# A decoder layer on one core: Strassen's gate over even and odd token tiles, the first weight tile in two column parts, buffers of gate, down and the out stage laid anew

## The chip, the core and the metric

The kernel runs on one core of one Trainium2 chip. The metric is the device time of one execution, in microseconds. Before the change the median of three runs is 3316.95 us (3312.92 to 3322.59).

## The reference

One layer of a decoder, for 1024 tokens of width 1024, all in float32: a SwiGLU block, a token mixer (an mLSTM branch and an RWKV-7 branch that two gates merge), and a second SwiGLU block, with a layer norm behind each.

```python
def swiglu(x, w_gate, w_up, w_down):
    return (jax.nn.silu(x @ w_gate) * (x @ w_up)) @ w_down
...
for l in range(DEPTH):
    x = layer_norm(ALPHA * x + 0.5 * swiglu(x, ffn1_w_gate[l], ffn1_w_up[l], ffn1_w_down[l]), ln1_g[l], ln1_b[l])
    mix = token_mixer(x, w_in[l], ...)
    x = layer_norm(ALPHA * x + mix, ln2_g[l], ln2_b[l])
    x = layer_norm(ALPHA * x + 0.5 * swiglu(x, ffn2_w_gate[l], ffn2_w_up[l], ffn2_w_down[l]), ln3_g[l], ln3_b[l])
```

The weights `w_gate` and `w_up` are 1024 x 2816 (22 column tiles of 128), `w_down` is 2816 x 1024.

## The kernel before, in words

**Numbers.** A float32 product is made of three fp32r products. `split` (L128) cuts a tile into a high part (a cast on ACT) and a low part (source minus high, on POOL or on DVE: `lo_eng`), and `mm3` (L148) issues high times high, high times low and low times high on TensorE (PE). So each operand costs a cast and a subtraction, and each product three matmuls, nearly all of 128x512.

**Stages.** In order of time: the gate of ffn1 (gate and up, to about 475 us), its down (to about 775), the mixer (B and C), the out stage D (`mix_out`, layer norm 2; about 2380 to 2562), the gate of ffn2 (to about 3034), its down with layer norm 3, and the end.

**The gate.** `gate_up` (L284) computes for one column tile f the gate and up of all tokens by Winograd's form of Strassen: the tokens in two halves (tiles 0 to 3 and 4 to 7) and the depth in two halves give a 2x2 block product with 7 products instead of 8, 84 matmuls instead of 96. The seven sums of token blocks are made once for a stage: `put_sums` (L222) adds and subtracts on DVE, and `put` (L211) transposes each sum on PE (L216, four 128x128 transposes), casts the high part on ACT (L219) and takes the low part from PSUM on DVE (L220). `weights` (L264) makes the seven sums of the weight blocks for each f (`tw` tiles, DVE, L266) and splits them, the low parts on POOL. The results come through `e` tiles: DVE adds (L288), a Silu on ACT, two products (L313, L318), and two 128x512 stores to h in DRAM (L315, L319). The stores go through SP's queue, those of the last f through ACT's. In both gates the first two products of the first two f's are "led" (`lead`): they need only the first half's plain blocks, and so run while the other sums are still being made.

**The down.** `down_all` (L355) takes the token tiles in groups of 3, 3 and 2. For each of the 22 f's it loads a piece of h (`hr`, L365) and two halves of a row block of `w_down` (`rw`, L371), splits them (`hr` with its low part on DVE, `rw` with its low parts on DVE and POOL in turn), and accumulates in PSUM. At a group's end DVE adds the sums to the residual (L390). The layer norms of a group (`layer_norm`, L420) are popped into the loop of the next group, one each third f; it works on pairs of tiles: statistics, a subtraction of the mean on ACT (L430), a product with gamma on POOL (L431), a chain of small DVE operations for the inverse root (L160 to L164, tiles `lnr` and `rst`), and a DVE operation of 128x1024 for each tile (L440). In the first down each normed tile is transposed too (`to_T`, L173 to L177).

**Buffers and queues.** `rw` (8), `tw` (6), `wr` (14) and `e` (18) are rings of 128x512 tiles. SP issues nearly all loads and stores in program order, and an entry whose buffer isn't free holds all behind it. The mixer's first loads of `w_in` (`raw`, `rawf`, L143) stand where their buffers let them, in before at the end of the first gate.

Of the kernel before, what the change touches and what calls it, by code (L numbers as in the profile page):

```python
# [16 lines left out]
P = 128  # L17
# [13 lines left out]
class Net:  # L31
    def __init__(self, ctx, tc, ins, out):
        self.ctx, self.tc, self.nc, self.I, self.out = ctx, tc, tc.nc, ins, out
        tp = lambda **kw: ctx.enter_context(tc.tile_pool(**kw))
        self.cp = tp(name="cp", bufs=1)
        self.gp = {}
        self.sp = self.rp = None
        self.pp = tp(name="pp", bufs=1, space=PSUM)
        self.dp = tp(name="dp", bufs=1, space=bass.MemoryType.DRAM)
        self.n = 0  # L40
# [7 lines left out]
    RING = {"rw": (8, F32), "tw": (6, F32), "wr": (14, F32R), "e": (18, F32)}  # L48
# [11 lines left out]
    def ring(self, tag, n=512):  # L60

        bufs, dt = self.RING[tag]
        return (self.ep if tag == "e" else self.rp).tile([P, 512], dt, tag=tag, bufs=bufs, name=self.nm(tag))[:, :n]
# [135 lines left out]
    def sums_pool(self, name):  # L199

        return self.pool(name)

    def sums(self, pool, a=None):
        big = lambda: pool.tile([P, NK, 512], F32R, tag="xq", bufs=3, name=self.nm("xq"))
        a, b = a or self.new_xT(), self.new_xT()
        c, d = (big(), big()), big()
        lo4, hi4 = slice(0, 4), slice(4, 8)
        return [self.cut(a, ALL, lo4), self.cut(a, ALL, hi4), self.cut(b, ALL, lo4), self.cut(b, ALL, hi4),
                self.cut(c, ALL, lo4), self.cut(c, ALL, hi4), (d[:, lo4], d[:, hi4])]
# [12 lines left out]
    def put_sums(self, cmb, a1, a2, s1):  # L222

        tt_ = self.nc.vector.tensor_tensor
        banks = "acdc"
        for p in range(4):
            tt_(s1[p], a2[p][0], a2[p][1], op=ALU.add)
            tt_(a2[p][0], a1[p][0], a2[p][0], op=ALU.subtract)
            tt_(a1[p][0], s1[p], a1[p][0], op=ALU.subtract)
            self.put(cmb[2], p, a1[p][0], banks[p])  # L230
        for i, t in ((3, lambda p: a2[p][0]), (4, lambda p: s1[p]), (5, lambda p: a2[p][1])):
            for p in range(4):
                self.put(cmb[i], p, t(p), banks[p])
        for p in range(4):
            tt_(a1[p][1], a1[p][1], a1[p][0], op=ALU.subtract)
            self.put(cmb[6], p, a1[p][1], banks[p])

    def prod(self, ps, w, x, first):
        for k in range(4):
            self.mm3(ps, self.cut(w, ALL, k), self.cut(x, ALL, k), first and k == 0, k == 3, not first)  # L240

    def lead(self, cmb, w1, w2):

        X, X2 = self.ps("g"), self.ps("b")
        self.prod(X, w1, cmb[0], True)
        self.prod(X2, w2, cmb[1], True)
        return X, X2

# [15 lines left out]
    def weights(self, b11, b12, b21, b22, led):  # L264
# [4 lines left out]
        if not led:  # L269
            out[0] = self.cut_w(b11)  # L270
# [3 lines left out]
        if not led:  # L274
            out[1] = self.cut_w(b21)
# [8 lines left out]
    def gate_up(self, cmb, f, ws, hD, led=None):  # L284
# [3 lines left out]
        add = lambda o, a, b: nc.vector.tensor_tensor(o, a, b, op=ALU.add)  # L288
        pr = lambda ps, i, first: self.prod(ps, ws[i], cmb[i], first)
        p1, sg0 = self.ring("e"), self.ring("e")  # L290
        if led:
            nc.scalar.copy(p1, led[0])
            add(sg0, led[1], p1)
            nc.scalar.activation(sg0, sg0, AF.Silu)
        else:
            X = self.ps("g")
            pr(X, 0, True)
            nc.scalar.copy(p1, X)
        u2, u3, up1, sg1, up0 = (self.ring("e") for _ in range(5))
        Y, Z = self.ps("b"), self.ps("c")  # L300
        pr(Y, 2, True)
        add(u2, Y, p1)
        if not led:
            pr(X, 1, False)
            nc.scalar.activation(sg0, X, AF.Silu)
# [8 lines left out]
        dma = (nc.scalar if f == NF - 1 else nc.sync).dma_start  # L314
        dma(hD[f * P:(f + 1) * P, 512:1024], up1)  # L315
# [3 lines left out]
        dma(hD[f * P:(f + 1) * P, 0:512], up0)  # L319

    def gate_first(self, pre, src, cmb, hD):

        nc = self.nc

        def get(r, c):
            ts = [self.ring("e") for _ in range(4)]
            for p in range(4):
                nc.sync.dma_start(ts[p], src[(4 * r + p) * P:(4 * r + p + 1) * P, c * 512:(c + 1) * 512])
            return ts

        B = [[None] * 4 for _ in range(2)]
        raws = lambda f, n, i: [B[f].__setitem__(i + 2 * k, self.raws(pre, f, k, (n,))[0]) for k in range(2)]
        a11 = get(0, 0)
        raws(0, "gate", 0)
        a12 = get(0, 1)
        raws(1, "gate", 0)
        a21 = get(1, 0)
        raws(0, "up", 1)
        a22 = get(1, 1)
        raws(1, "up", 1)  # L340
        for p in range(4):
            self.put(cmb[0], p, a11[p], "acdc"[p])
        for p in range(4):
            self.put(cmb[1], p, a12[p], "acdc"[p])
        led = [self.lead(cmb, self.cut_w(B[f][0]), self.cut_w(B[f][2])) for f in range(2)]
# [1023 lines left out]
```

## Time and profile before

| what | value |
|---|---|
| median of three runs | 3316.95 us |
| the profiled execution | 3316.42 us, its span 3314.7 us |
| mean granted TensorE clock | 0.967 |
| PE busy | 3100.1 us (94%) |
| DVE, ACT, POOL busy | 1984.5, 1085.7, 998.1 us |
| steady gate, 128x512 matmuls in 100 us | 432 |

The span is nearly the sum of PE's work and of the gaps in it, so it is read by its gaps: how long PE is idle in each stage, and what ended each wait. In the view by stretches each engine has its busy time and its number of instructions; in the view of waits a row names the waiting engine, the tile and line that waited, what released it, and the sum, count and longest of the waits.

### The profile page before, as it was taken

How to read it: one execution, taken by the hardware profiler on the slowest of the kernel's cores; microseconds unless marked ns; L12 is line 12 of the kernel's file. 1: busy time of each engine (PE TensorE's matmuls, PEld its weight loads, DVE VectorE, ACT ScalarE, POOL GpSimd, SP SyncE). 2: the span in 40 equal slices, each digit the busy share in tenths (PEclk: the TensorE clock that was granted, in tenths of full speed). 3: DMA queues.
4: the chain of work that ended last, by engine and by line, in shares of the span. 5: the costliest groups of instructions: out<-in, count | busy, mean ns of one | idle time of the engine just before them, and what ended most of it. 6: DMA issues, size and time to landing. Idle time of an engine off the chain costs nothing. (4 is left out here: it accounts for less than half of the span.)

```text
span 3314.7 us, 44985 instructions
## 1 busy us (share of the span) xinstructions
PE 3100.1 (94%) x15720; PEld 2495.2 (75%) x15720; DVE 1984.5 (60%) x4654; ACT 1085.7 (33%) x1790; POOL 998.1 (30%) x975
## 2 busy tenths in 40 slices
PE   7999989988899899999989999999999699999997
PEld 5888867777677777787877777777777588887785
DVE  6444435674657666757576766476568744444658
ACT  4333323443312222313232322375333333333434
POOL 3444433343212222222222122200002344443334
PEclk9999999999989999999998999999999899999998
DMA  3222237552222322322232223474562322224564
GB/s 121 80 86 83 77 107 234 185 189 66 58 69 64 77 78 57 78 60 76 66 73 64 74 77 93 129 234 143 178 232 83 108 82 77 80 86 156 167 200 164
DMA packets 457001, 365.37 MB, mean 110 GB/s; under 512 B 109981, under 2 KB 368711, under 8 KB 456775
## 3 DMA queue, kind: packets, MB, share of 16 engines
q1 hardware_dynamic: 449287, 348.87, 35.2%
q0 software_dynamic: 4608, 8.39, 0.9%
q10 hardware_dynamic: 2880, 5.24, 0.4%
q8 instruction: 124, 2.03, 0.3%
q14 instruction: 102, 0.84, 0.1%
HBM read 281.66 MB, written 80.74 MB: 109 GB/s over the span
## 5 line engine op out<-in xcount | busy, mean ns | idle before, releaser
L150 PE MATMUL psg<-xT,wf 128*128 128x512 f32 x2340 | 641.5, 410 | 0.7 <-ACT f L871 0.7
L134 POOL TENSOR_TENSOR wr<-rw,wr 128x512 fp32r<-128x512 f32 x260 | 345.2, 1328 | 511.2 <-ACT wr L130 450.4
L150 PEld LDWEIGHTS psg<-xT,wf 128*128 128x128 f32 x2340 | 429.1, 192 | 76.4 <-ACT f L871 1.1
L130 ACT CAST wr<-rw 128x512 fp32r<-128x512 f32 x392 | 242.1, 621 | 497.0 <-PE psc L150 253.5
L150 PE MATMUL psa<-xT,w 128*128 128x512 f32 x1200 | 316.4, 406 | 13.7 <-DVE pj L507 10.6
L134 POOL TENSOR_TENSOR wr<-tw,wr 128x512 fp32r<-128x512 f32 x176 | 233.9, 1331 | 303.6 <-ACT wr L130 303.6
L150 PE MATMUL psb<-xT,wr 128*128 128x512 f32 x1080 | 271.3, 401 | 15.6 <-ACT wr L130 10.7
L150 PEld LDWEIGHTS psa<-xT,w 128*128 128x128 f32 x1200 | 222.7, 192 | 64.8 <-DVE pj L507 15.3
L288 DVE TENSOR_TENSOR e<-psb,e 128x512 f32<-128x512 f32 x136 | 94.0, 691 | 293.3 <-PE psb L150 293.3
L150 PE MATMUL psc<-xq,wr 128*128 128x512 f32 x1056 | 260.5, 395 | 0.0
L150 PEld LDWEIGHTS psb<-xT,wr 128*128 128x128 f32 x1080 | 206.1, 191 | 66.6 <-ACT wr L130 11.5
L150 PE MATMUL psg<-wr,wr 128*128 128x512 f32 x792 | 213.9, 403 | 36.5 <-DVE wr L134 14.9
L150 PE MATMUL psg<-xT,wr 128*128 128x512 f32 x984 | 243.3, 396 | 1.5 <-ACT xT L219 1.5
L150 PEld LDWEIGHTS psc<-xq,wr 128*128 128x128 f32 x1056 | 199.4, 189 | 46.3
L150 PEld LDWEIGHTS psg<-xT,wr 128*128 128x128 f32 x984 | 186.1, 189 | 44.8 <-ACT xT L219 1.9
L130 ACT CAST wr<-tw 128x512 fp32r<-128x512 f32 x176 | 108.7, 621 | 327.1 <-PE psb L150 231.5
L150 PE MATMUL psb<-wr,wr 128*128 128x512 f32 x792 | 212.1, 405 | 0.0
L150 PEld LDWEIGHTS psg<-wr,wr 128*128 128x128 f32 x792 | 150.5, 192 | 75.3 <-DVE wr L134 18.8
L134 DVE TENSOR_TENSOR wr<-hr,wr 128x384 fp32r<-128x384 f32 (+1 forms) x132 | 163.7, 1240 | 47.6 <-ACT wr L130 41.4
L134 POOL TENSOR_TENSOR wf<-rawf,wf 128x512 fp32r<-128x512 f32 x100 | 133.3, 1349 | 179.2 <-ACT wf L130 154.3
L150 PEld LDWEIGHTS psb<-wr,wr 128*128 128x128 f32 x792 | 156.2, 198 | 33.7
L134 DVE TENSOR_TENSOR wr<-rw,wr 128x512 fp32r<-128x512 f32 x132 | 100.6, 762 | 134.2 <-PE psc L150 107.8
(369 smaller groups left out, 5190.6 us busy)
## 6 DMA issues: line engine op xcount, KB each, us to landing
rw<-in_ffn_w_down_dram SPq DMA_DIRECT2D x264, 256.0 KB
rawf<-in_w_in_dram SPq DMA_DIRECT2D x98, 256.0 KB
rw<-in_ffn_w_gate_dram SPq DMA_DIRECT2D x88, 256.0 KB
rw<-in_ffn_w_up_dram SPq DMA_DIRECT2D x88, 256.0 KB
h<-e SPq DMA_DIRECT2D x84, 256.0 KB
hr<-h SPq DMA_DIRECT2D x88, 192.0 KB
raw<-in_w_in_dram SPq DMA_DIRECT2D x50, 256.0 KB
qkD<-f SPq DMA_DIRECT2D x32, 256.0 KB
```

Of the source, the lines that this page charges most:

```text
L130: nc.scalar.copy(hi, src)
L134: eng.tensor_tensor(lo, src, hi.bitcast(F32), op=ALU.subtract)
L150: self.nc.tensor.matmul(out, a[u], b[v], start=first and i == 0, stop=last and i == 2, skip_group_check=more)
L288: add = lambda o, a, b: nc.vector.tensor_tensor(o, a, b, op=ALU.add)
```

## The change

What it does:

- Strassen's token halves are the even and the odd tiles instead of the first and the last four. `put_sums` then works for one pair of tiles at a time: four DVE sums and seven transposed sets for a pair.
- The first f of each gate is computed in two column parts: columns 0 to 255 (pairs 0 and 1) and 256 to 511 (pairs 2 and 3). In the first gate the second two pairs are loaded and summed after the first part in program order. The led products are gone.
- h is stored in pieces of 128x128, eight DMAs for an f instead of two, since the halves are interleaved in h.
- The ring of `e` has 14 buffers instead of 18; `wr` has a pool of its own in the first gate and another in the first down; `lng`, `hr` and `lnb` get their places at the start of the down.
- In the down both low parts of `rw` are taken on DVE; POOL takes none. The product with gamma moves from POOL to DVE, for all three layer norms.
- The mixer's first `w_in` loads are issued after the load of `w_down` for f = 17 of the third group.
- D: the eight `y` tiles have a pool of their own, `unit` tiles go from 18 to 10, gamma and beta are loaded at D's start, nothing is led, and no tile is transposed in the layer norm's callback; `put_sums` runs for the four pairs after `mix_out`.

The diff, cut to its core:

```diff
-    RING = {"rw": (8, F32), "tw": (6, F32), "wr": (14, F32R), "e": (18, F32)}
+    RING = {"rw": (8, F32), "tw": (6, F32), "wr": (14, F32R), "e": (14, F32)}
...
-    def put_sums(self, cmb, a1, a2, s1):
+    def put_sums(self, cmb, p, a1, a2, s1):
         tt_ = self.nc.vector.tensor_tensor
...
+        self.put(cmb[0], p, a1[0], "a")
+        tt_(s1, a2[0], a2[1], op=ALU.add)
+        tt_(a2[0], a1[0], a2[0], op=ALU.subtract)
+        self.put(cmb[1], p, a1[1], "c")
+        tt_(a1[0], s1, a1[0], op=ALU.subtract)
+        self.put(cmb[2], p, a1[0], "d")
+        self.put(cmb[3], p, a2[0], "c")
+        tt_(a1[1], a1[1], a1[0], op=ALU.subtract)
+        self.put(cmb[4], p, s1, "a")
+        self.put(cmb[5], p, a2[1], "c")
+        self.put(cmb[6], p, a1[1], "d")
...
-        dma = (nc.scalar if f == NF - 1 else nc.sync).dma_start
-        dma(hD[f * P:(f + 1) * P, 512:1024], up1)
+        hv = hD[f * P:(f + 1) * P, :].rearrange("r (p e t) -> r e p t", e=2, t=P)
+        dma = (nc.scalar if f == NF - 1 else nc.sync).dma_start
+
+        def store(e, t):
+            for p in range(c0 // P, c1 // P):
+                dma(hv[:, e, p], t[:, p * P - c0:(p + 1) * P - c0])
...
+        pair(0)
+        pair(1)
+        ws = self.weights(*B)
+        self.gate_up(cmb, 0, ws, hD, 0, 256)
+        pair(2)
+        pair(3)
+        self.gate_up(cmb, 0, ws, hD, 256, 512)
+        self.gate_rest(pre, cmb, hD, 1)
...
+            if f == 0:
+                self.gate_up(cmb, f, ws, hD, 0, 256)
+                self.gate_up(cmb, f, ws, hD, 256, 512)
...
+                    if (t0, f) == (6, 17):
+                        self.loaded = dma
                     d = self.ring("wr"), self.ring("wr")
-                    self.split(raw, *d, lo_eng=("dve", "pool")[c])
+                    self.split(raw, *d, lo_eng="dve")
...
-        nc.gpsimd.tensor_tensor(y[tt], y[tt], gb, op=ALU.mult)
+        nc.vector.tensor_tensor(y[tt], y[tt], gb, op=ALU.mult)
...
-    with net.phase("D", UB=18, VB=5, side="right"):
-        net.mix_out(net.hmT, y, fin2, load_y, load_ln)
-        a = x2T[0]
-        led = [net.lead([net.cut(a, ALL, k) for k in k4], *(net.cut(w, ALL, k) for k in k4)) for w in led]
+    with net.phase("D", UB=10, VB=5, side="right"):
+        load_ln()
+        v = [net.half() for _ in range(5)]
+        yt = [net.s("y", [P, D], bufs=8) for _ in range(8)]
+        y.extend(yt[4:] + yt[:4])
+        net.mix_out(net.hmT, y, fin2, load_y)
...
+            for p in range(4):
+                net.put_sums(cmb, p, *([y[2 * p + e][:, c] for c in c2] for e in range(2)), net.half())
...
-        net.rwkv_small(x1T)
-        with net.low():
-            for f in net.fillers(x1T):
-                f()
+        with tc.issue_after(net.loaded.ins):
+            net.rwkv_small(x1T)
+            with net.low():
+                for f in net.fillers(x1T):
+                    f()
```

How the program's order moves, at three places. The first is SP's queue at the very start, behind the first loads of x (`e`) and weights (`rw`); before:

```order
L328 DMA e_122<-in_x_dram 128x512
L328 DMA e_123<-in_x_dram 128x512
L328 DMA e_124<-in_x_dram 128x512
L328 DMA e_125<-in_x_dram 128x512
L253 DMA rw_130<-in_ffn_w_up_dram 128x4x128
L253 DMA rw_132<-in_ffn_w_up_dram 128x4x128
L328 DMA e_134<-in_x_dram 128x512
L328 DMA e_135<-in_x_dram 128x512
L328 DMA e_136<-in_x_dram 128x512
L328 DMA e_137<-in_x_dram 128x512
```

and after the change, where 13 to 18 of the queue are the weights of f = 1 and two small loads, and these follow:

```order
L241 DMA rw_762<-in_ffn_w_gate_dram 128x4x128
L241 DMA rw_764<-in_ffn_w_up_dram 128x4x128
L241 DMA rw_766<-in_ffn_w_gate_dram 128x4x128
L241 DMA rw_768<-in_ffn_w_up_dram 128x4x128
L284 DMA h_77<-e_270 128x128 x2
L315 DMA e_374<-in_x_dram 128x512
L284 DMA h_77<-e_272 128x128 x2
L315 DMA e_375<-in_x_dram 128x512
L315 DMA e_376<-in_x_dram 128x512
L315 DMA e_377<-in_x_dram 128x512
```

The x of pairs 2 and 3 (`e_374` on) now stands behind the third tile's weights, which wait for ring buffers of the first, and behind the first part's stores of h, which wait for its results.

The second place is SP's queue between the first gate and its down; `raw` and `rawf` are the mixer's weights, `hr` the pieces of h that the down starts with. Before:

```order
L371 DMA rw_3784<-in_ffn_w_down_dram 128x512
L319 DMA h_77<-e_3414 128x512
L143 DMA raw_6277<-in_w_in_dram 128x4x128
L143 DMA raw_6281<-in_w_in_dram 128x4x128
L143 DMA rawf_6287<-in_w_in_dram 128x4x128
L143 DMA rawf_6291<-in_w_in_dram 128x4x128
L143 DMA raw_10177<-in_w_in_dram 128x4x128
L365 DMA hr_3664<-h_77 128x384
```

and after:

```order
L284 DMA h_77<-e_3618 128x128 x4
L358 DMA rw_4024<-in_ffn_w_down_dram 128x512
L284 DMA h_77<-e_3620 128x128 x4
L352 DMA hr_3904<-h_77 128x384
L352 DMA hr_3940<-h_77 128x384
L352 DMA hr_3976<-h_77 128x384
```

The five `w_in` loads are gone from in front of the first `hr`.

The third place is DVE in the third token group of the second down, where the layer norm of the group before is woven between the splits (L134). Before:

```order
L440 SCALAR_TENSOR_TENSOR u_26361<-u_26361,lnr_27656,lnb_26067 128x1024
L440 SCALAR_TENSOR_TENSOR u_27211<-u_27211,lnr_27656,lnb_26067 128x1024
L134 TENSOR_TENSOR wr_27748<-hr_27745,wr_27747 128x256
L163 SCALAR_TENSOR_TENSOR rst_27873<-rst_27873,lnv_27870 128x2
L164 SCALAR_TENSOR_TENSOR lnr_27871<-rst_27873,lnr_27871 128x2
L134 TENSOR_TENSOR wr_27754<-rw_27751,wr_27753 128x512
```

and after:

```order
L429 SCALAR_TENSOR_TENSOR u_26837<-u_26837,lnr_28132,lnb_26543 128x1024
L429 SCALAR_TENSOR_TENSOR u_27687<-u_27687,lnr_28132,lnb_26543 128x1024
L134 TENSOR_TENSOR wr_28236<-rw_28233,wr_28235 128x512
L420 TENSOR_TENSOR u_27689<-u_27689,lng_26541 128x1024
L134 TENSOR_TENSOR wr_28263<-hr_28260,wr_28262 128x256
L416 BN_AGGR lnmv_28239<-lnst_28338 128x2
L418 TENSOR_SCALAR lnn_28342<-lnmv_28239 128x1
L425 TENSOR_SCALAR lnv_28346<-lnmv_28239 128x2
L134 TENSOR_TENSOR wr_28269<-rw_28266,wr_28268 128x512
```

DVE now has the second low part of each f (`rw`, 128x512) and the product with gamma (L420, 128x1024) in its row.

More of the change, by code (lines that the diff above doesn't have):

```diff
@@ L191, in bcast_row, with big, halves @@
         return t
[L199 to L209, printed above, removed]
+    def big(self, pool):
+        return pool.tile([P, NK, 512], F32R, tag=self.nm("xq"), bufs=1, name=self.nm("xq"))
+    @staticmethod
+    def halves(hl):
+        return [tuple(t[:, 4 * c:4 * c + 4] for t in hl) for c in range(2)]
     def put(self, cmb, p, t, bank):
@@ L220, in put, with prod @@
         nc.vector.tensor_tensor(lo, p3, hi.bitcast(F32), op=ALU.subtract)
-    def put_sums(self, cmb, a1, a2, s1):
+    def put_sums(self, cmb, p, a1, a2, s1):
         tt_ = self.nc.vector.tensor_tensor
[L225 to L238, printed above, removed]
-        for k in range(4):
[L240 to L247, printed above, removed]
+        self.put(cmb[0], p, a1[0], "a")
[9 more added lines that the diff above has]
+        self.put(cmb[6], p, a1[1], "d")
+    def prod(self, ps, w, x, first, cs):
+        for k in range(4):
+            self.mm3(ps[:, cs], self.cut(w, ALL, k), self.cut(x, ALL, k, cs), first and k == 0, k == 3, not first)
     def raws(self, pre, f, k0, names=("gate", "up")):
@@ L262, in cut_w, with weights @@
         return [x.rearrange("p (k c) -> p k c", c=P) for x in hl]
[L264 removed]
+    def weights(self, b11, b12, b21, b22):
         sub = lambda o, a, b: self.nc.vector.tensor_tensor(o, a, b, op=ALU.subtract)
@@ L268, in weights @@
         out = {}
-        if not led:
-            out[0] = self.cut_w(b11)
+        out[0] = self.cut_w(b11)
         sub(t1, b12, b11)
@@ L273, in weights @@
         out[2] = self.cut_w(t2)
-        if not led:
-            out[1] = self.cut_w(b21)
+        out[1] = self.cut_w(b21)
         sub(t3, b22, b12)
@@ L318, in gate_up @@
         nc.vector.scalar_tensor_tensor(up0, sg0, 0.5, up0, op0=ALU.mult, op1=ALU.mult)
-        dma(hD[f * P:(f + 1) * P, 0:512], up0)
+        store(0, up0)
     def gate_first(self, pre, src, cmb, hD):
         nc = self.nc
[L325 to L345, printed above, removed]
@@ L346, in gate_first, with pair @@
-        s1 = [self.ring("tw") for p in range(4)]
-        self.put_sums(cmb, list(zip(a11, a12)), list(zip(a21, a22)), s1)
-        self.gate_rest(pre, cmb, hD, led, B)
-    def gate_rest(self, pre, cmb, hD, led, B=None):
-        for f in range(NF):
-            b = B[f] if B and f < 2 else self.raws(pre, f, 0) + self.raws(pre, f, 1)
-            l = led[f] if f < 2 else None
-            self.gate_up(cmb, f, self.weights(*b, l is not None), hD, l)
+        B = []
+        def pair(p):
+            a = [[self.ring("e") for _ in range(2)] for _ in range(2)]
+            for e in range(2):
+                for c in range(2):
+                    nc.sync.dma_start(a[e][c], src[(2 * p + e) * P:(2 * p + e + 1) * P, c * 512:(c + 1) * 512])
+            if p < 2:
+                B.extend(self.raws(pre, 0, p))
+            self.put_sums(cmb, p, *a, self.ring("tw"))
@@ L360, in down_all @@
         y, late = [], []
+        if self.wp is self.sp:
+            self.ring("wr")
+        for tag, shape, bufs in (("lng", [P, D], 1), ("hr", [P, 384], 4), ("lnb", [P, D], 1)):
+            self.s(tag, shape, bufs=bufs)
         for t0, n in ((0, 3), (3, 3), (6, 2)):
```

84 lines of the change are left out of this document (39 added, 45 removed).

## The prediction

> **What bounds the kernel now.** I read the profile in this order: the busy times by stage, then the waits of PE in the stages where it is idle, then the timelines of PE, SP's queue and DVE at those waits. The view by stretches, for PE, PEld, DVE, ACT and POOL in turn:
>
> ```profile
> core 0: us, PE busy (x) PEld busy (x) DVE busy (x) ACT busy (x) POOL busy (x), PEclk, DMA share, GB/s
> 0.00:86.00 86.00, 66.42 (x288) 51.31 (x289) 58.66 (x79) 33.97 (x57) 33.57 (x40) 0.92 0.39 118
> 86.00:474.00 388.00, 388.00 (x1671) 314.95 (x1671) 155.42 (x209) 115.09 (x193) 172.32 (x134) 1.00 0.25 79
> 484.00:774.00 290.00, 265.47 (x1130) 214.59 (x1130) 194.58 (x248) 121.67 (x220) 118.83 (x93) 0.95 0.58 186
> 800.00:2380.00 1580.00, 1492.50 (x8851) 1200.87 (x8849) 1027.15 (x3361) 485.54 (x773) 331.27 (x465) 0.97 0.34 91
> 2380.00:2562.00 182.00, 166.67 (x704) 130.91 (x705) 128.78 (x198) 56.33 (x79) 21.21 (x10) 0.97 0.47 159
> 2562.00:2650.00 88.00, 60.92 (x268) 47.35 (x268) 69.91 (x105) 29.92 (x49) 32.85 (x21) 0.84 0.32 99
> 2650.00:3034.00 384.00, 384.00 (x1654) 311.70 (x1653) 154.54 (x208) 113.72 (x191) 170.77 (x132) 1.00 0.25 79
> 3034.00:3298.00 264.00, 249.71 (x1057) 203.05 (x1057) 173.77 (x212) 112.49 (x204) 102.76 (x72) 0.96 0.61 200
> ```
>
> In the two steady gates PE is busy without a gap. The first has 20 tiles of 84 matmuls in 388 us, so one tile takes 19.4 us and one matmul 0.231 us (the records that the count lacks are the few that a trace can lose). Nothing of the change shortens that. The mixer's 87.5 idle us (1580 less 1492.5) are left as they are, since its instructions stand in the same order. What the change can touch is PE's idle time in the other stages: 19.6 at the start, about 11.5 at the first seam (below), 24.5 in the first down, 15.3 in D, 27.1 behind D, 14.3 in the second down. That makes some 112 us, an upper bound of any gain. What ends these waits, in the view of waits (sum, count, longest), from the start, the seam of gate and down, the first down, its end, the seam behind D, and the second down, ahead of it the timeline's row of the second seam:
>
> ```profile
> PE psb L150 <- DVE e L288: 4.6, 2, 4.1
> ...
> PE psg L150 <- ACT wr L130: 9.7, 1, 9.7
> PE psg L150 <- DVE wr L134: 1.8, 1, 1.8
> ...
> PE psg L150 <- DVE wr L134: 7.1, 4, 2.9
> PE psg L150 <- POOL wr L134: 2.7, 2, 2.5
> ...
> PE psa L173 <- DVE u L440: 7.0, 1, 7.0
> ...
> PE psa L216 <- DVE u L229: 8.7, 1, 8.7
> PE psb L150 <- ACT wr L130: 7.6, 1, 7.6
> ...
> 3037.69 0.49 PE L150 MATMUL psg<-wr,wr 128*128 128x512 f32 x1 [2.99 <-ACT wr L130]
> ...
> PE psg L150 <- DVE wr L134: 5.7, 3, 2.4
> PE psg L150 <- POOL wr L134: 5.2, 2, 2.7
> ```
>
> **First seam.** ACT, SP's queue and PE there:
>
> ```profile
> 474.14 0.34 ACTq L315 DMA_DIRECT2D h<-e  x1
> ...
> 474.80 1.00 SPq L143 DMA_DIRECT2D raw<-in_w_in_dram  x2
> ...
> 479.86 0.37 SPq L143 DMA_DIRECT2D raw<-in_w_in_dram  x1
> 480.27 0.98 SPq L365 DMA_DIRECT2D hr<-h  x2
> ...
> 483.41 0.51 ACT L130 CAST wr<-hr 128x384 fp32r<-128x384 f32 x1
> ...
> 484.49 0.80 PE L150 MATMUL psg<-wr,wr 128*128 128x512 f32 x1 [9.73 <-ACT wr L130]
> ```
>
> The last load of `w_in` waits for its buffer until 479.86, and the first `hr` behind it issues at 480.27, lands, and is cast at 483.41, 3.1 us after its issue; PE starts 1.1 us behind that, 9.73 behind the gate's end (474.76). With the loads gone `hr` waits only for the stores of h in front of it, whose last come through ACT's queue. Such a store is issued at 474.14; I take its way at two us, an estimate below the 3.1 of `hr`. So `hr` is issued at 476.4, cast at 479.5, and PE starts at 480.6; the second wait of 1.8 shrinks to 0.4. The gap goes from 11.5 to about 6: **−5.5** (bounds −8 and −2). ACT's eight store issues at 0.34 us, 2.7 us in all, lie under that wait; where it is gone they cost about 1 us. **Second seam:** there nothing stood in front of `hr` before, and PE waited 2.99. The same eight pieces now lie in front, as at the first: 3 to 6, **+3** (bounds 0 and +5).
>
> **Column parts.** The trace has a 256-column matmul of this form in the mixer, and this row of one run of them; beside it the start's cold and warm groups of twelve:
>
> ```profile
> 1332.19 4.23 PE L150 MATMUL psg<-wf,xT 128*128 128x256 f32 x34
> ...
> 62.25 4.57 PE L150 MATMUL psb<-xq,wr 128*128 128x512 f32 x12 [4.11 <-DVE e L288]
> ...
> 69.45 2.95 PE L150 MATMUL psb<-xT,wr 128*128 128x512 f32 x12
> ```
>
> 4.23 us for 34 is 0.124 us each, so 168 halves take 20.9 us against 19.4: at most +1.5 for each gate. It is within the terms of the start and of D's seam. A group that follows a gap of 4.1 us takes 4.57 instead of 2.95, so each such gap costs 1.6 us beyond itself.
>
> **The start.** The view of DVE and POOL by groups and of single operations gives the prices (the first row from behind D, the others from DVE's `put` there and from the third group of the second down):
>
> ```profile
> L266 DVE TENSOR_TENSOR tw<-rw,rw 128x512 f32<-128x512 f32 x9 | 11.6, 1285 | 2.6 <-DMA rw<-in_ffn_w_up_dram 2.1 <-POOL wr L134 0.6
> ...
> 2591.28 0.68 DVE L220 TENSOR_TENSOR xq<-psa,xq 128x512 fp32r<-128x512 f32 x1
> 2591.88 0.68 DVE L220 TENSOR_TENSOR xq<-psc,xq 128x512 fp32r<-128x512 f32 x1
> ...
> L134 DVE TENSOR_TENSOR wr<-hr,wr 128x256 fp32r<-128x256 f32 x20 | 23.9, 1197 | 4.3 <-ACT wr L130 4.3
> L134 DVE TENSOR_TENSOR wr<-rw,wr 128x512 fp32r<-128x512 f32 x21 | 15.8, 753 | 4.3 <-PE psb L150 3.6 <-DMA hr<-h 0.7
> L440 DVE SCALAR_TENSOR_TENSOR u<-u,lnr,lnb 128x1024 f32<-128x1024 f32 x4 | 8.1, 2052 | 0.1
> ...
> L134 POOL TENSOR_TENSOR wr<-rw,wr 128x512 fp32r<-128x512 f32 x20 | 27.7, 1385 | 26.7 <-ACT wr L130 22.4 <-issue 4.3
> L431 POOL TENSOR_TENSOR u<-u,lng 128x1024 f32<-128x1024 f32 x3 | 8.1, 2702 | 5.0 <-ACT u L430 5.0
> ```
>
> A `put` costs DVE 0.60 us (start to start), as does a sum that is not disturbed. Pairs 0 and 1 need 14 sets and 8 sums, 13 us, and their weights seven low parts on POOL at 1.39, 10 us; with the first loads the first part's products end at about 36 us. Only then, behind its stores of h, are the x of pairs 2 and 3 issued: about 37, with some 3 us to land. PE idles about 4 us. Then 22 DVE operations at 0.62 and the casts before them take about 16 us, to 56; the rest of the second part (about 51 halves) is 6 us, and f = 1 is 19.4: it ends near 82. Before it ended at 474.8 less 20 tiles of 19.44, at 86: **−3**. From both sides: −6 if the second part's products keep up with the sums; +5 if the loads come at 42 or the sums are slowed. On the latter the trace says that the `tw` sums, with two operands in SBUF, take 1.29 us on the mean beside POOL's splits, while `put`, which reads PSUM, takes 0.68 undisturbed. The Trainium skill, on its page "SBUF — State Buffer" (section "SBUF: two separate sides"), says that a DVE operation with two inputs in SBUF and a GpSimd operation exclude each other for the whole instruction. By that rule alone all eight sums of pairs 2 and 3, which now fall into POOL's weight splits, would wait for a split each, at most 8 x 0.7 = 5.6 us, and the start's term would be about +2 (an estimate from that page's rule). The row's mean, twice the undisturbed one, agrees with the rule where POOL is busy; but POOL is idle for part of that stretch, so I keep −3.
>
> **The downs.** POOL leaves them. In the third group DVE's `hr` operation took 1.20 us on the mean, and the normal's L440 2.05. The same operations alone:
>
> ```profile
> 3238.06 0.41 DVE L134 TENSOR_TENSOR wr<-hr,wr 128x256 fp32r<-128x256 f32 x1
> ...
> 3308.51 2.48 DVE L440 SCALAR_TENSOR_TENSOR u<-u,lnr,lnb 128x1024 f32<-128x1024 f32 x2
> ```
>
> So 0.79 us go for each of some 20 `hr`, 0.8 for each L440, and nearly all of the stretch of the small chain operations. Against this come 20 low parts at 0.69 and three products with gamma at 1.28 (like L440): removed 20 x 0.79 + 4 x 0.8 = 19, added 20 x 0.69 + 3 x 1.28 = 17.6. DVE's sum stays; but it now comes in one row, with no POOL operation of 2.7 in front of a low part. PE's waits for POOL (2.7 and 5.2) go; those for DVE (7.1 and 5.7) stay about, since in the third group the norm of three tiles still stands among the splits: evictions 4 us, norm some 17, splits 1.55 for each f over nine f's, less about one and a half f's done ahead: 33 us, in which PE has some 22 us of work and 4 us ahead, so a stall of 7 as before. In sum **−3** for the first down and **−2** for the second (bounds −10 and +5 each).
>
> **End of the first down.** PE waits 7.0 for the last norm; gamma on DVE saves a turn to POOL (2.7 against 1.28 for each of two tiles, 2.6 less). But the first splits of `w_in` now come in the last f's and this tail: **−1** (bounds −3 and +3). The same saving at the kernel's end, where the last norm ends the span: **−1**.
>
> **D and its seam.** Within D I leave the waits as they are: gamma adds 8 x 1.28 = 10 us on DVE, which is busy 129 of 182 us, and the transposes of four tiles leave (bounds ±5). Behind D 23 of the 28 sets, 16 sums and the norm of the last pair remain: 23 x 0.60 + 16 x 0.62 + 9 = 33 us of DVE. With waits the products start at 37, f = 0 takes 20.9, f = 1 19.4 and the cold start 2: f = 2 starts 79 us behind D. In the trace it starts 20 tiles of 19.44 before the gate's end at 3034.7, at 2645.8, which is 84 behind: **−4** (bounds −9 and +5). The led products, that filled PE before, are the price: without them nothing covers the first 37 us.
>
> **The sum.** −3 −5.5 −3 −1 −4 +3 −2 −1 = −16.5 on the profiled execution's 3316.4 gives 3299.9; the median lies 0.5 above that execution. I forecast **3300.5**.
>
> **The rivals.** *Full relief* (chance 0.14): if POOL's lock of DVE, not the amount of DVE's work, makes the downs' waits, then 7.1 + 2.7 + 5.7 + 5.2 = 20.7 go instead of 5: 3285. For it speaks the `hr` row at three times its own length; against it that DVE is still busy 33 of the third group's first 30-odd us by my count. The page named above would have it so. *Given back* (0.27): the start comes out at +2 for the late x or the locked sums, the downs at 0, the second seam at +5: 3300.5 + 5 + 5 + 2 = 3312.5, no change that can be told. For it speaks the order of SP's queue, which puts loads behind results. *DVE the bound* (0.12), on the other side: with both low parts, gamma and, in the first down, the transposes' low parts on one in-order engine, the third groups fall behind. DVE's 34 us of splits, 20 of norm, 4 of evictions and 5 of transposes are 63 against 61 us of PE (22 x 12 x 0.231); it decides from the point where DVE's work up to the norm's end exceeds PE's by more than the `wr` ring holds ahead. At 8 us more a down, with 5 more in D and the start at +5, it is 3300.5 + 16 + 5 (the gains lost) + 5 + 8 = 3334. Against it speaks that 17 us of that row's work lies in the first nine f's only.
>
> **Chances.** My forecast has 0.47, with a range of its own from 3292 to 3310. A measurement of this kernel tells about 0.3% (10 us) from no change, that is below 3307 for faster. Faster: 0.14 + 0.43 + 0.03 from the second rival = 0.60. Same: 0.04 + 0.22 = 0.26. Slower: 0.12 + 0.02 = 0.14. The range reaches to both nearer rivals: 3284 to 3322.
>
> **What would show it.** Right: the gap at the first seam near 6 us, the second's near 6, `hr` at 0.45 to 0.55 on DVE in the downs and no POOL there, f = 2 of the second gate 79 us behind D, the first gate steady from 82. Wrong: PE waits at the start for `e<-in_x_dram` over 8 us; waits for `wr` on DVE of over 10 us in a third group; a steady gate above 19.5 us for a tile, which would mean that the eight small stores or the shorter `e` ring hold it; or a change in the mixer, which I take to have none.

## The result and the profile after

The changed kernel takes 3261.9 us (median of four runs, 3257.9 to 3264.6), against 3319.8 for the kernel before on the same chips: a ratio of 0.9827, with an interval from 0.9806 to 0.9848. It is faster by some 58 us. The forecast was 3300.5 us (3284 to 3322): the sign was right, the size less than a third of it.

The two profiled executions, cut at the same events, show where the 55.6 us between their spans (3314.7 and 3259.1) lie. The tiles f = 2 to 21 of each gate are its steady part.

| stretch | before | after | difference | forecast |
|---|---|---|---|---|
| start, to the end of f = 1 | 84.2 | 89.3 | +5.1 | −3 |
| steady first gate, 20 tiles | 390.4 | 380.8 | −9.6 | 0 |
| first seam | 9.7 | 5.1 | −4.6 | −5.5 |
| first down, first to last matmul | 277.5 | 256.2 | −21.3 | −3 |
| to the last norm's transposes | 12.6 | 9.3 | −3.3 | −1 |
| mixer, to D's start | 1608.4 | 1596.0 | −12.4 | 0 |
| D, to its last product | 178.6 | 182.0 | +3.4 | 0 |
| seam behind D, f = 0 and 1 | 82.3 | 84.8 | +2.5 | −4 |
| steady second gate, 20 tiles | 390.4 | 390.4 | 0 | 0 |
| second seam | 3.0 | 5.1 | +2.1 | +3 |
| second down | 260.7 | 244.9 | −15.8 | −2 |
| end | 16.3 | 14.5 | −1.8 | −1 |

The view by stretches of the changed kernel (times of PE, PEld, DVE, ACT and POOL with their instructions, then the granted clock, DMA's share and GB/s), for the start, 80 us of the first gate, the first down with the wait behind it, the mixer, D, the seam behind it, 80 us of the second gate, and the second down:

```profile
0.00:90.00 90.00, 65.46 (x368) 57.58 (x369) 56.55 (x83) 34.13 (x60) 31.34 (x39) 0.89 0.39 111
90.00:170.00 80.00, 80.00 (x355) 66.24 (x354) 33.98 (x46) 24.95 (x42) 38.63 (x30) 1.00 0.29 83
475.00:741.00 266.00, 257.92 (x1131) 210.10 (x1132) 174.39 (x323) 124.10 (x225) 16.04 (x24) 0.98 0.66 209
741.00:2337.00 1596.00, 1517.79 (x8950) 1219.94 (x8950) 1036.08 (x3375) 498.52 (x793) 335.18 (x468) 0.97 0.34 92
2337.00:2519.00 182.00, 165.90 (x685) 128.53 (x685) 123.40 (x206) 51.54 (x70) 0.00 (x0) 0.95 0.44 150
2519.00:2606.00 87.00, 65.49 (x355) 56.31 (x354) 63.68 (x110) 32.05 (x56) 29.19 (x21) 0.82 0.30 92
2620.00:2700.00 80.00, 80.00 (x346) 64.87 (x345) 33.78 (x46) 24.66 (x42) 36.63 (x30) 1.00 0.28 79
2999.00:3245.00 246.00, 243.03 (x1056) 198.74 (x1056) 150.78 (x283) 111.92 (x204) 0.00 (x0) 0.99 0.65 212
```

POOL has gone from the downs but for 16 us at the end of the first (12 of `w_in` splits, the rest fills of the mixer's buffers), and PE is idle for 3 us in the second down instead of some 11. Two rows hold something that no step of the forecast had: both gates are busy without a gap at a granted clock of 1.00, yet in the same 80 us the first runs 355 matmuls and the second 346. The kernel before ran 346 in both:

```profile
90.00:170.00 80.00, 80.00 (x346) 64.93 (x345) 33.21 (x46) 24.27 (x41) 37.54 (x29) 1.00 0.27 83
2660.00:2740.00 80.00, 80.00 (x346) 64.97 (x345) 33.81 (x46) 24.61 (x42) 36.65 (x30) 1.00 0.26 79
```

From one matmul's start to the next it is 226 or 227 ns in the first gate after the change, and 228 to 241 (mean 232.4) in the others. 1680 matmuls by 5.7 ns are the 9.6 us of the table.

The waits of PE in the two downs after the change, first and second, each with the seam ahead of it:

```profile
PE psg L150 <- ACT wr L130: 6.3, 2, 5.1
PE psg L150 <- DVE wr L134: 2.6, 4, 0.8
```

```profile
PE psg L150 <- ACT wr L130: 5.1, 1, 5.1
PE psg L150 <- DVE wr L134: 2.2, 4, 1.0
```

Before, the first down without its seam had these:

```profile
PE psg L150 <- DVE wr L134: 8.9, 5, 2.9
PE psg L150 <- POOL wr L134: 2.7, 2, 2.5
PE psa L173 <- DVE u L440: 2.6, 1, 2.6
PE psa L173 <- DVE xT L177: 2.5, 3, 1.4
PE psg L150 <- ACT wr L130: 0.9, 1, 0.9
```

The waits for POOL are gone, and so are most of those for DVE, which the forecast had kept. DVE's groups in the third token group of the second down:

```profile
L134 DVE TENSOR_TENSOR wr<-rw,wr 128x512 fp32r<-128x512 f32 x44 | 29.9, 688 | 12.3 <-ACT wr L130 12.0
L134 DVE TENSOR_TENSOR wr<-hr,wr 128x256 fp32r<-128x256 f32 x21 | 8.8, 418 | 0.0
...
L429 DVE SCALAR_TENSOR_TENSOR u<-u,lnr,lnb 128x1024 f32<-128x1024 f32 x4 | 4.9, 1278 | 0.0
L420 DVE TENSOR_TENSOR u<-u,lng 128x1024 f32<-128x1024 f32 x3 | 3.6, 1213 | 0.0
```

`hr` fell from 1197 to 418 ns, the norm's last operation from 2052 to 1278, each to its length alone. Even with 23 more low parts and three products with gamma, DVE has room: it waits 12 us in this stretch for ACT.

The start went wrong, in part as its rival said. SP's queue, then PE, then single operations of DVE, after the change:

```profile
36.47 0.83 SPq L284 DMA_DIRECT2D h<-e  x2
37.38 0.38 SPq L315 DMA_DIRECT2D e<-in_x_dram  x1
37.86 0.86 SPq L284 DMA_DIRECT2D h<-e  x2
38.81 3.32 SPq L315 DMA_DIRECT2D e<-in_x_dram  x7
```

```profile
40.47 0.81 PE L212 MATMUL psa<-ident,e 128*128 128x128 f32 x4 [3.96 <-DMA e<-in_x_dram]
42.19 1.11 PE L212 MATMUL psc<-ident,e 128*128 128x128 f32 x4 [0.91 <-DMA e<-in_x_dram]
46.07 1.09 PE L212 MATMUL psa<-ident,tw 128*128 128x128 f32 x4 [2.77 <-DVE tw L222]
...
67.80 2.66 PE L150 MATMUL psb<-xq,wr 128*128 128x256 f32 x12 [1.97 <-DVE e L275]
...
89.29 2.88 PE L150 MATMUL psg<-xq,wr 128*128 128x512 f32 x12
```

```profile
45.23 0.69 DVE L222 TENSOR_TENSOR tw<-e,e 128x512 f32<-128x512 f32 x1 [0.58 <-DMA e<-in_x_dram]
...
63.95 1.78 DVE L254 TENSOR_TENSOR tw<-rw,rw 128x512 f32<-128x512 f32 x1
65.78 1.63 DVE L254 TENSOR_TENSOR tw<-rw,tw 128x512 f32<-128x512 f32 x1
67.33 0.41 DVE L275 TENSOR_TENSOR e<-psb,e 128x256 f32<-128x256 f32 x1
```

The x of pairs 2 and 3 is issued from 37.4 on, behind the first stores, and PE waits 3.96 us for its first block, as the working had it. But PE waits 0.91 and 2.77 us more: the first sum of pair 2 still waits for x, and starts at 45.23. The later wait of 1.97 is for an `L275` that stands in DVE's row behind long sums of weight blocks (L254). f = 2 starts at 89.3, not at 82.

### The profile page after: what moved, and what is told of

Same layout as the page of the kernel before. It is cut to its first block, busy times and chain, and to the rows that moved or that the text cites. A ratio compares the mean times of both kernels' runs of the same rounds, so it can differ in the third digit from the quotient of the medians.

```text
span 3259.1 us, 45659 instructions
## 1 busy us (share of the span) xinstructions
PE 3084.5 (95%) x15888; PEld 2500.5 (77%) x15888; DVE 1928.2 (59%) x4820; ACT 1085.7 (33%) x1796; POOL 757.2 (23%) x819
## 3 DMA queue, kind: packets, MB, share of 16 engines
q8 instruction: 125, 2.05, 0.3%
## 5 line engine op out<-in xcount | busy, mean ns | idle before, releaser
L150 PE MATMUL psg<-xT,wf 128*128 128x512 f32 x2328 | 632.1, 407 | 0.7 <-ACT f L860 0.7
L134 POOL TENSOR_TENSOR wr<-tw,wr 128x512 fp32r<-128x512 f32 x176 | 229.2, 1304 | 264.2 <-ACT wr L130 258.3
L134 DVE TENSOR_TENSOR wr<-rw,wr 128x512 fp32r<-128x512 f32 x264 | 182.9, 699 | 178.7 <-ACT wr L130 167.6
L134 POOL TENSOR_TENSOR wr<-rw,wr 128x512 fp32r<-128x512 f32 x132 | 173.7, 1316 | 493.9 <-ACT wr L130 493.8
L275 DVE TENSOR_TENSOR e<-psb,e 128x512 f32<-128x512 f32 (+1 forms) x138 | 92.2, 668 | 296.6 <-PE psb L150 296.6
L150 PE MATMUL psb<-xq,wr 128*128 128x512 f32 (+1 forms) x1104 | 260.7, 386 | 6.5 <-DVE e L275 4.8
L150 PE MATMUL psc<-xq,wr 128*128 128x512 f32 (+1 forms) x1104 | 259.1, 384 | 1.5 <-DVE e L275 1.5
L150 PEld LDWEIGHTS psb<-xq,wr 128*128 128x128 f32 x1104 | 204.7, 192 | 48.5 <-issue 3.0
L134 POOL TENSOR_TENSOR w<-raw,w 128x512 fp32r<-128x512 f32 (+1 forms) x51 | 65.3, 1294 | 491.9 <-ACT w L130 430.6
L134 POOL TENSOR_TENSOR wf<-rawf,wf 128x512 fp32r<-128x512 f32 x98 | 129.7, 1339 | 166.9 <-ACT wf L130 151.6
L774 POOL TENSOR_SCALAR S<-S,PC 128x128 f32<-128x128 f32 x120 | 80.2, 668 | 292.6 <-DVE S L776 181.4
L150 PE MATMUL psc<-wr,wr 128*128 128x512 f32 x528 | 134.2, 389 | 0.0
```

Source lines behind the costliest of these rows:

```text
L134: eng.tensor_tensor(lo, src, hi.bitcast(F32), op=ALU.subtract)
L150: self.nc.tensor.matmul(out, a[u], b[v], start=first and i == 0, stop=last and i == 2, skip_group_check=more)
L275: add = lambda o, a, b: nc.vector.tensor_tensor(o, a[:, cs], b, op=ALU.add)
L774: nc.gpsimd.tensor_scalar(S1, S, pcn, None, op0=ALU.mult)
```

## The experiments

Theories. *Lock*: a POOL operation that reads SBUF holds up DVE's operations on two SBUF operands, and through them PE; the change gains because no POOL operation runs in the downs. *Data path*: PE waits for POOL's own slow low part. *Buffers*: the new places and the new order of tiles make the gain.

**One low part back on POOL**, in the changed kernel:

```diff
-                    self.split(raw, *d, lo_eng="dve")
+                    self.split(raw, *d, lo_eng=("dve", "pool")[c])
```

> The changed kernel, with only the low parts of the down's second weight half back on POOL. In the two profiles the downs' matmuls take 256 and 243 us after the change against 277 and 259 before. Lock theory (a POOL operation keeps DVE's two-operand SBUF operations waiting, and with them PE): both downs lose most of this again, 25 to 37 us, 3287 to 3299. Data-path theory (PE waits for the slow low part itself, behind gamma on POOL): since gamma is now on DVE, 5 to 15, 3267 to 3277. Buffer theory (places of the tiles and order make the gain): within 5 of the changed kernel, 3262 to 3267.

3285.7 us, 0.989 of before (0.9875 to 0.9905): 24 us of the gain are gone. The downs take 271.2 and 252.4. The second down's third group, DVE and then POOL:

```profile
L134 DVE TENSOR_TENSOR wr<-hr,wr 128x256 fp32r<-128x256 f32 x20 | 22.9, 1146 | 4.0 <-ACT wr L130 4.0
...
L429 DVE SCALAR_TENSOR_TENSOR u<-u,lnr,lnb 128x1024 f32<-128x1024 f32 x4 | 7.1, 1796 | 0.0
```

```profile
L134 POOL TENSOR_TENSOR wr<-rw,wr 128x512 fp32r<-128x512 f32 x21 | 30.3, 1441 | 37.9 <-ACT wr L130 25.9 <-DVE wr L134 6.4 <-DVE lnst L415 3.6
```

`hr` is at 1146 again. That speaks against buffers, but 24 us lie a little below the lock's range and above the data path's.

**A POOL operation that nobody reads**, in the changed kernel; the splits stay on DVE:

```diff
                     self.split(raw, *d, lo_eng="dve")
+                    if c:
+                        nc.gpsimd.tensor_tensor(self.s("junk", [P, 512], mybir.dt.bfloat16, bufs=1), raw, raw, op=ALU.subtract)
```

> The changed kernel, with one more POOL subtraction of 128x512 for each f of the downs whose result nobody reads (source the raw weights twice, result a scratch tile in bf16); the splits stay on DVE. Lock theory: POOL's operation alone, without any data path to PE, brings back 20 to 37 us, 3282 to 3299, and DVE's hr low part is again near 1.2 us on the mean. Data-path and buffer theories: no change beyond 5 us, 3260 to 3267.

3283.3 us, 0.9889 (0.9874 to 0.9903), with downs of 268.0 and 254.9. No data goes from POOL to PE here, and the loss is that of the run above. In the third group, DVE and POOL, then PE's waits in the whole second down:

```profile
L134 DVE TENSOR_TENSOR wr<-rw,wr 128x512 fp32r<-128x512 f32 x42 | 35.3, 856 | 4.1 <-ACT wr L130 3.9
L134 DVE TENSOR_TENSOR wr<-hr,wr 128x256 fp32r<-128x256 f32 x21 | 11.7, 555 | 0.0
...
L364 POOL TENSOR_TENSOR junk<-rw 128x512 bf16<-128x512 f32 x18 | 25.3, 1408 | 38.1 <-DMA rw<-in_ffn_w_down_dram 38.1
```

```profile
PE psg L150 <- DVE wr L134: 9.7, 10, 2.1
```

The expectation missed in one point: `hr` rose to 555 ns only. POOL's operation now starts when the raw weights land, and it is `rw`'s low part that it hits (688 to 856). Which operation waits depends on when POOL starts; that DVE waits does not.

**Gamma back on POOL**, in the changed kernel:

```diff
-        nc.vector.tensor_tensor(y[tt], y[tt], gb, op=ALU.mult)
+        nc.gpsimd.tensor_tensor(y[tt], y[tt], gb, op=ALU.mult)
```

> The changed kernel, with only gamma's product back on POOL, in all three layer norms. Lock theory: the few POOL operations of 2.4 us hit the norm's chain and the splits around it, so the second down loses 5 to 10 of its 16 us, the first 3 to 8, the end of the first down and of the kernel 1.5 to 3 each: in sum 10 to 20 more, 3270 to 3280. Rival (gamma's place is worth only its own time at the two ends): 3 to 5 more, 3264 to 3267.

3302.8 us, 0.9959 (0.9943 to 0.9974): 41 us more than the changed kernel, twice the upper end of what was expected, from eight operations of 2.4 us in each norm. The downs take 268.2 and 255.5, the wait behind the first 12.6 again, D 188.7, the mixer 1602, the end 16.5. So 22.6 of the 41 us lie in the two downs, about what the low parts cost there (22.5 in the first run); 12 lie behind the first down, in D and at the end, where gamma stands in the norm's own chain; and 6 are the mixer's, whose code is the same. POOL and DVE in the third group of the second down:

```profile
3222.18 2.40 POOL L420 TENSOR_TENSOR u<-u,lng 128x1024 f32<-128x1024 f32 x1 [86.07 <-ACT u L419]
```

```profile
3221.90 0.69 DVE L415 BATCH_NORM_STATS2 lnst<-u 128x6 f32<-128x512 f32 x1
3222.51 2.10 DVE L162 TENSOR_TENSOR rst<-lnr 128x2 f32<-128x2 f32 x1
3224.53 0.68 DVE L415 BATCH_NORM_STATS2 lnst<-u 128x6 f32<-128x512 f32 x1
3225.13 0.14 DVE L163 SCALAR_TENSOR_TENSOR rst<-rst,lnv 128x2 f32<-128x2 f32 x1
```

A DVE operation of two elements in a partition, 0.15 us alone, lasts until 3224.61, and POOL's ends at 3224.58. All of DVE's row stands behind it. The Trainium skill, on its page "SBUF — State Buffer" (section "SBUF: two separate sides"), has this as an exclusive lock for the whole instruction; the trace agrees.

**The kernel before with its low parts on DVE**, gamma still on POOL:

```diff
-                    self.split(raw, *d, lo_eng=("dve", "pool")[c])
+                    self.split(raw, *d, lo_eng="dve")
```

> The kernel before, with only the low parts of the down moved to DVE, gamma still on POOL. Lock theory: nearly the whole gain of the downs, 25 to 35 us, 3285 to 3295 against 3320. Data-path theory: 5 to 15 less. Buffer theory: no gain, or a loss of up to 10, since DVE then has all low parts in the old buffers.

3301.3 us, 0.9952 (0.9934 to 0.9971): 20 us less than before, below the lock's range, since gamma remains. The downs take 263.1 and 255.6.

**The kernel before with low parts and gamma on DVE**: the line above, and

```diff
-        nc.gpsimd.tensor_tensor(y[tt], y[tt], gb, op=ALU.mult)
+        nc.vector.tensor_tensor(y[tt], y[tt], gb, op=ALU.mult)
```

> The kernel before, with the low parts and gamma on DVE, so with no POOL operation in the downs and the old buffers. Lock theory: both downs as after the change, 256 and 244 us with 2 us to spare, 3278 to 3286. Buffer theory of what the low parts alone left (the second down at 255.6 against 244.9): downs of 260 and over 250, 3290 to 3300.

3265.0 us, 0.9845 (0.9827 to 0.9862). Two words of code give some 52 us, nearly all that the whole change gives. The downs take 255.4 and 244.6 in the old buffers, as after the change, and D with its seam and the second gate 644.6 where before it was 651.3 and after the change 657.2. So the new D, with its seam and the cut first tile, costs some 13 us against the old one with gamma on DVE. PE's waits in the second down with its seam:

```profile
PE psg L150 <- ACT wr L130: 3.0, 1, 3.0
PE psg L150 <- DVE wr L134: 2.2, 4, 1.0
```

The row of DVE is that of the changed kernel to the tenth. So the buffers of the downs are worth nothing that shows here, and the buffer theory falls.

**The first tile of the second gate in one piece**, in the changed kernel:

```diff
-            if f == 0:
-                self.gate_up(cmb, f, ws, hD, 0, 256)
-                self.gate_up(cmb, f, ws, hD, 256, 512)
-            else:
-                self.gate_up(cmb, f, ws, hD)
+            self.gate_up(cmb, f, ws, hD)
```

> The changed kernel, with the first tile of the second gate in one piece of 512 columns instead of two. In the changed kernel's profile this tile takes 29.4 us against 19.4 of a whole one. Theory of short groups (products of 1.45 us do not cover the turn of PSUM through ACT and DVE, and each gap cools the clock): 4 to 8 us less, 3254 to 3258. Rival (the weights' low parts on POOL or the cold clock set the tile's length, not its cutting): within 2 us of the changed kernel.

3253.9 us, 0.9816 (0.9785 to 0.9846). From D's last product to the end of the gate it takes 470.4 instead of 475.2, so the two parts cost 4.8. In the changed kernel, two short products and what came between (products are groups of 12):

```profile
2565.56 1.58 PE L150 MATMUL psc<-xq,wr 128*128 128x256 f32 x12
2569.94 2.75 PE L150 MATMUL psb<-xq,wr 128*128 128x256 f32 x12 [2.81 <-DVE e L275]
2572.50 2.06 PE L150 MATMUL psc<-xq,wr 128*128 128x256 f32 x12
```

A product of 1.58 us does not cover what DVE does between two uses of the same PSUM, and the next one runs cold (2.75 us). But the whole tile has this wait too (2.92 us). In both, the `L275` that PE waits for stands in DVE's row behind three or four sums of weight blocks, most of them 1.6 to 1.8 us long beside POOL's splits, where one alone takes 0.68. The cut tile waits a second time (1.51 us), and without its waits takes 24.8 us to the whole one's 22.2, since more of it runs cold. In all the cut tile took 29.4 us, not 20.9, and the whole one 25.1.

**Without the rule on `w_in`**, in the changed kernel:

```diff
-        with tc.issue_after(net.loaded.ins):
-            net.rwkv_small(x1T)
-            with net.low():
-                for f in net.fillers(x1T):
-                    f()
+        net.rwkv_small(x1T)
+        with net.low():
+            for f in net.fillers(x1T):
+                f()
```

> The changed kernel without the rule that holds the mixer's first w_in loads back. First seam: 9 to 11 us instead of 5.1. The mixer from the first transposes to D's start took 1608.4 and 1608.7 us with the old layout and 1591 to 1597 with the new one, with the same instruction order on ACT and DVE. If the rule makes that difference: about 1608 here, in sum 3275 to 3280. If the mixer's gain comes from elsewhere (places of tiles): the mixer stays at 1591 to 1597 and the sum is 3264 to 3269.

3258.1 us, 0.982 (0.9802 to 0.9838): no slower than the changed kernel. The seam has its long wait again, in the row of PE's waits around it:

```profile
PE psg L150 <- ACT wr L130: 9.9, 1, 9.9
```

but the first down takes 253.8 instead of 256.2, and the mixer 1594.6. What the seam gained was half given back within the down: in the changed kernel POOL's eight held splits of `w_in` run at 711.8 to 728.4 us, in the down's third group, and without the rule five of them run in the seam.

**The same rule in the kernel before**: `self.loaded` is set at the load for (6, 17), and the mixer's first calls stand in `tc.issue_after(net.loaded.ins)`.

> The kernel before, with only the rule that holds the mixer's first w_in loads back. First seam 5 to 6 instead of 9.7 us, less 4 to 6 in sum; the mixer at 1608 if its gain comes from elsewhere (3314 to 3317), or at 1591 to 1597 if this rule makes it (3300 to 3306).

3319.1 us, 0.9998 (0.998 to 1.0016): no change. The seam shrank by 6.6 us, and the first down grew from 277.5 to 281.9. The mixer took 1603.8, between the two expectations, which doesn't decide.

**The new first gate in the kernel before**: both operations on DVE as above, and in the first gate pairs, two parts and small stores; rings, `wr`'s place, D and the second gate are the old ones.

```diff
+        pair(0)
+        pair(1)
+        ws = self.weights(*B, False)
+        self.gate_up(cmb, 0, ws, hD, None, 0, 256, True)
+        pair(2)
+        pair(3)
+        self.gate_up(cmb, 0, ws, hD, None, 256, 512, True)
```

> The kernel before with both POOL operations on DVE (as in the run of both), and only the first gate as after the change: even and odd tiles, pairs, the first tile in two parts, small stores; D, its seam and the second gate as before, with led products. The first gate ends at 470 instead of 477; D with its seam and the second gate takes 645 us as in that run, against 657 after the change and 652 with the whole first tile. The mixer at 1608 to 1611 as in all kernels with the old layout so far: 3257 to 3262. If the first gate's buffers are what shortens the mixer to 1591 to 1597: 3244 to 3249.

3254.4 us, 0.9803 (0.9777 to 0.9829). The first gate ended at 479.3, not at 470: its products start as in the changed kernel, but a matmul takes 232.4 ns. So the new start itself is no gain, and the faster matmul comes from neither the tiles' order nor the stores. D with its seam and the second gate took 638.1, less than the 645 expected, and 19 less than the changed kernel's. The mixer took 1599, between the two expectations.

**Both small edits**: the whole first tile, and no rule on `w_in`, in the changed kernel, as in the two diffs above.

> The changed kernel with the second gate's first tile in one piece and without the rule that holds w_in back. If the two act apart: 3254 less 0 to 4, so 3250 to 3255. If the rule's gain at the first seam counts in full: 3258 to 3260.

3256.8 us, 0.9817 (0.9795 to 0.9839): within the intervals of either alone. What the rule is worth is too little for these medians to tell.

**Where the weights lie.** In the built kernel before, `wr` lies in the first gate at 188 to 217 KB of a partition (counted in thousands of bytes), and the operands that stream past at 20 to 135; after the change the first gate has `wr` at 20 to 49 and the operands behind it, to 164; the second gate has `wr` at 201 to 229 and the operands at 20 to 135 in both. One run moves `wr` down to 135 to 164 in the second gate (together with the whole first tile); one moves it up to 172 to 201 in the first, where the operands then lie at 20 to 135:

```diff
-            net.wp = net.rp
-            with net.pool("E2", "right") as net.ep:
+            with net.pool("W2") as net.wp, net.pool("E2", "right") as net.ep:
...
             with net.phase("F", UB=6, side="right"):
+                net.wp = net.sp
```

> The changed kernel with the second gate's first tile in one piece, and wr of the second gate in a pool of its own on the lower side (as the first gate has it after the change), wr of the second down in that stage's pool. In the changed kernel one 128x512 matmul follows another after 226.7 ns in the first gate and 232.4 in the second; before the change both had 232.4. Place theory (where the weights' tiles lie sets this): 227 in the second gate too, 1700 x 5.7 ns = 9.6 us less than the whole first tile alone, 3243 to 3246. Rival (something else of the first stage, its even and odd tiles or its small stores): 232 in the second gate, 3252 to 3255.

```diff
-            with net.pool("W1") as net.wp, net.pool("X1") as xp, net.pool("E1", "right") as net.ep:
+            with net.pool("W1", "right") as net.wp, net.pool("X1") as xp, net.pool("E1", "right") as net.ep:
```

> The changed kernel with one word more: wr's pool of the first gate on the upper side of SBUF, where the old kernel's rings lie, instead of the lower; sizes and order as they were. Place theory: 232 ns a matmul in the first gate, 9.6 us more than the changed kernel, 3270 to 3273. Rival (a pool of its own is enough, or the cause is elsewhere): 227 ns, 3260 to 3264.

The view by stretches, 80 us of the first and of the second gate, with the second gate's weights low:

```profile
100.00:180.00 80.00, 80.00 (x355) 66.24 (x354) 33.80 (x47) 24.89 (x42) 37.52 (x29) 1.00 0.29 83
2640.00:2720.00 80.00, 80.00 (x355) 66.24 (x354) 33.48 (x46) 24.95 (x42) 38.31 (x30) 1.00 0.30 86
```

and with the first gate's weights high:

```profile
100.00:180.00 80.00, 80.00 (x344) 64.35 (x343) 32.94 (x46) 23.90 (x40) 37.44 (x29) 1.00 0.29 82
2640.00:2720.00 80.00, 80.00 (x346) 64.86 (x345) 33.10 (x46) 24.19 (x41) 37.51 (x29) 1.00 0.29 83
```

The first of the two takes 3248.4 us, 0.9782 (0.9748 to 0.9817), the lowest median of all; D's seam and second gate take 460.4 where 470.4 stood. The second takes 3269.7 us, 0.9855 (0.9826 to 0.9883), and its first gate ends at 480.0 instead of 470.1. Its first seam took 9.1 us for 5.1, and its mixer 1587.7, so the median tells less than the 10 us of the gate. The place of the weights' tiles sets the rate, both ways: in the first run the streamed operand stays where it was. Within the slow places the rate is 232.4 or 233.3 ns, and the kernel before had the one in its first profile and the other in its second (below), so that difference is not the place's. In the downs both operands come from one ring, at 132 to 161, 188 to 217 or 201 to 229, and their warm matmuls run at 227. What it is about the places that costs the time was not tried.

**Both kernels once more**, for the mixer's length alone; nothing is changed in either.

> The kernel before once more, for the mixer alone: from the first transposes to D's start it took 1608.4, 1608.7 and 1610.5 us in three kernels with the old code up to there, and 1588 to 1602 in those with the new first gate. If each program has its own length: 1606 to 1611. If the length is drawn anew in each execution: anything from 1588 to 1611.

> The changed kernel once more, for the mixer alone (1596.0 in its first profile). If each program has its own length: 1593 to 1599. If it is drawn anew in each execution: anything from 1588 to 1611.

The mixer took 1608.5 us in the one and 1592.3 in the other, against 1608.4 and 1596.0. PE's idle time in it was 88.6 and 78.1 us, against 91.0 and 78.2: as far as two executions of each can show, it belongs to the program, though the order of PE's instructions is the same. PE's busy time in the mixer is not so fixed: over all runs it goes from 1507 to 1524 us, with the granted clock from 0.976 to 0.963.

## Why the prediction was right or wrong

*The downs* are the step that failed: "DVE's sum stays", so "those for DVE (7.1 and 5.7) stay about", and with that −3 and −2 us for what measured −21.3 and −15.8. DVE's sum did not stay: in the second down it fell from 173.8 to 150.8 us, with all the new work in it. The working set the new low parts against the waiting operations of the third group, where its prices were right (1.20 to 0.42 for `hr`, 2.05 to 1.28 for the norm's last step), but it named the stretch of the small chain operations without putting it into the sum. Nor did it ask what the 44 larger `hr` operations of the first two groups would save: they fell from 1.28 to 0.55 us. And a sum does not show that an operation that waits 2 us at the head of the row holds up all behind it. PE's waits fell from 11.1 to 2.2 us in the second down, and from 17.6 to 3.8 in the first.

The waits are only part of it. A cold restart was priced (1.6 us for a gap), but not put into the downs' sum. Beyond 226.7 ns each, the 1056 matmuls of the second down took 10.5 us before and 3.5 after, at granted clocks of 0.96 and 0.99; those of the first took 15.0 and 7.9. So about 9 of the 15.8 us are waits and 7 are pace, and in the first down 14 and 7 of the 21.3.

The rival of full relief had the mechanism, and was given 0.14. Its price, 20.7 us, left out the same cold clock, and counted 9.8 of the first down's 17.6 us of waits: the rows of the norm's transposes (L173) were left out. The runs with an idle POOL operation and with gamma show that the wait itself, and not POOL's result, is what counts.

*Gamma* was priced at its own time at two ends, 1 us each. Put back alone in the changed kernel it cost 41 us, 22.6 of them in the downs.

*The steady gates* were held to be untouched ("Nothing of the change shortens that"). The first lost 9.6 us to the place of its weights' tiles, which no step considered.

*The start* was +5.1 for −3. The loads behind the stores were issued as worked out (at 37), but their landing was sized too small: 4 us of waiting were counted, and PE waited 7.6, since the first sum of pair 2 started only at 45.2. Of the rival's two reasons the late x came true. The locked sums did not: the eight sums of pairs 2 and 3 took 0.69 us each, with POOL idle until 54.7. The sums of weight blocks behind them were held up instead (1.37, 1.78 and 1.63 us beside POOL's splits), and with them PE for 2 us, with 12 cold halves of 2.66 behind it. So the second part and f = 1 ended at 89, not at 82: the upper bound of the term, and beyond the rival's +2. The base was misread too: a tile is 84 times 232.4 ns, 19.5 us and not 19.44, so f = 2 started before the change at 84.2, not at 86, and in the second gate at 2644.1, not at 2645.8.

*D's seam* was +2.5 for −4: the products started 36 us behind D, as worked out at 37, and the first tile took 29.4 for 20.9, the term that failed, since halves were priced at full pace and without waits. D itself was +3.4, within its bounds; but with gamma on DVE alone the old D took 177.2 where the new one takes 182.0.

*Seams*: −4.6 for −5.5 and +2.1 for +3, right in mechanism and size; yet against the run without the rule, half of what the first one gains comes back as a longer down (256.2 for 253.8). *The two ends* were −3.3 and −1.8 for −1 and −1, the first just outside its bounds.

*The mixer*, −12.4 for 0, is not settled. PE's busy time in it is the same (1517.4 and 1517.8 us); what fell is its idle time, from 91.0 to 78.2. It is not the rule on `w_in` (80.4 without it), nor POOL's work in the downs (86.1 in the old kernel with both operations on DVE). It comes with the first gate: every kernel with the old first gate idles 85 to 91 us in the mixer, every one with the new one 77 to 80, and the old kernel in which, besides the two operations, only the first gate is new, 77.9. In that pair of kernels the mixer's instructions have the same order and the same places in SBUF; only the two buffers of `psg` and of `psc` in PSUM have changed turns. So places in SBUF are not the cause there, and the cause stays open. Between the kernels before and after, the fall lies in two places: about 1240 to 1275 us, where PE no longer waits 4.5 us for DVE, and in the last 170 us of it.

## What to carry to other kernels

Before pricing an edit that takes an engine out of a stage, look for operations that last far longer than the same form alone: a two-element DVE operation of 2 us beside a POOL operation of 2.4 is a wait, and on an in-order engine it is a wait for all that stands behind it. Price a wait of TensorE with the cold products behind it. And where a stage is bound by matmuls without gaps, compare its start-to-start time with that of another stage of the same form: here 5.7 ns in 232 were a matter of where a pool lay.

## What the runs showed of the hardware that was not expected

A few long POOL operations cost as much as many short ones beside the same DVE row: six products with gamma of 2.4 us in each down cost 22.6 us in the two downs together, 66 low parts of 1.4 us in each 22.5. The matmul's rate in fp32r depends on the place in SBUF of the weights against the streamed operand. It is 226.7 ns with the weights at 20 to 49 thousand bytes and the streamed operand at 49 to 164, or with the weights at 135 to 164 and the streamed operand at 20 to 135. With the streamed operand there and the weights at 172 to 229 it is 232.4 to 233.3. The granted clock is 1.00 in all these gates.
